# Four probability tiles, two loads moved behind a copy, a gate half copied by GpSimd, and the final scaling issued behind a maximum

## The chip, the cores and the metric

One core of a Trainium2 chip runs the kernel. The metric is the device time of one execution in microseconds. Engines are named as in the profile: PE is TensorE (matmuls; PEld its weight loads), DVE is VectorE, ACT is ScalarE, POOL is GpSimd, and SP is the engine whose queue issues most of the DMAs.

## The reference

One adaLN-modulated layer over 2048 latent tokens of width 1024 with 256 context tokens. All inputs are float32.

```python
h  = rms_norm(x) * (1 + scale) + shift          # scale, shift, gate from silu(c) @ w_ada + b_ada
rq, rk, rv, rg, aq, ak, av, ag = project(h, w_in)    # one combined projection, rope on rq rk aq ak
# group A, 4 heads of 128: retention over chunks of 128, forward (with the diagonal) and backward, summed;
#   y = group_norm(out_f + out_b) * gn_w * silu(rg)
# group B, 8 query heads of 64 on 2 key heads: window of +-128 keys and all 256 context keys, a sink logit:
m = max(max(logits), sink); p = exp(logits - m)
att = (p / (sum(p) + exp(sink - m))) @ v * silu(ag)
x = x + gate * (concat([ret, att]) @ w_out)
return rms_norm(x) * final_norm_w
```

## The kernel before

The first 660 us project all tokens in four groups of 512 and put queries, keys, values, gates and retention states into scratch in DRAM (`d_qkv`, `d_aq`, `d_k`, `d_v`, `d_g`, `d_st`). The work that this document is about comes after: a loop over 16 blocks of 128 tokens, two steps to a block, one for each group of four query heads (`kv` 0 and 1; step t is block t // 2, kv t % 2).

What happens to one attention head (`att_head`, `att_norm`, `att_t`, `att_v`): PE computes its scores S, 128 queries by up to 640 keys, into the single buffer of the pool `pS`. DVE adds the mask and takes the row maximum in one instruction (L759; listed as ISA in the instruction order and as CUSTOM_DVE in the profile), writing the scores to a tile `p` in SBUF. ACT takes the exponential with the row sum (L768), DVE the reciprocal (L777), POOL scales (L778), and a DMA on SP's queue (L782) copies the tile into `pr`, which holds four heads; the change calls this the copy. One step later PE transposes `pr` (L1212) into banks of tag t, ACT and DVE split each bank into a high and a low part `phl` (L1214, L1215), and PE multiplies by the values (`o`, L1225). In names such as `p_1_3` the first number is kv and the second the head in it; `S_0` to `S_7` number all eight heads of a block. The heads of a step belong to the next step's attention, so scores run one step ahead.

The other pieces of a step are retention (`ret_queries` on POOL, `ret_scores`, `ret_values`, `ret_moments`, `ret_norm`, `ret_rows`, `ret_out`), the output projection in eight pieces (`piece`, `proj`: three matmuls for each of the four slices of a half, L1262, then the residual sum by DVE, L1267), `att_out` (ACT's `ob`, DVE's `mf`, POOL's `ma`), `final_sum` (ACT squares the residual row, POOL makes the reciprocal root `rz`) and `final` (DVE scales by `rz` and the norm weights, L1286, and SP stores). `STEPS` lists the pieces of an even and an odd step in program order: a head's scores are a0 to a3, their scaling N0 to N3, transposes T, values V, projection o0 to o7, final sum f, final scaling F0 and F1. A scheduler reorders instructions of an engine around that list by its own priorities; a block under `behind(i)` keeps its instructions after `i` on the engine of `i`. Every engine then works through its own list strictly in that order, SP's queue of DMAs too.

At the hand-over, the last projection unit `ag1` of group 0 runs with the eight heads and the retention of block 0 woven into it (`WEAVE`). Its two results are copied out of PSUM into `glast` so that the projection's PSUM banks become free for the loop's (L1191); `last_gate` later applies silu to `glast`, stores it to `d_g`, and reads a quarter of it back as the upper half of block 0's gate `GA[0]`. `load_qkv`, `load_st`, `load_gr`, `load_kv`, `load_att` and `load_late` (gate `ga` and residual input `xb`) prefetch for later blocks, and `fw` holds the final norm's weights.

Of the kernel before, what the change touches and what calls it, by code (L numbers as in the profile page):

```python
# [8 lines left out]
F32 = mybir.dt.float32  # L9
F32R = mybir.dt.float32r  # L10
BF16 = mybir.dt.bfloat16
AF = mybir.ActivationFunctionType
ALU = mybir.AluOpType
# [3 lines left out]
P = 128  # L17
# [5 lines left out]
GT = 512  # L23
# [4 lines left out]

STEPS = (
    "a0 o0 O o1 a1 N0 o2 T0 r0 T1 r1 U a2 N1 V0 o3 T2 Y V1 o4 a3 N2 T3 V2 o5 q T4 N3 o6 V3 S o7 f V4",  # L30
    "a0 o0 O o1 a1 N0 R T0 F0 F1 a2 N1 T1 B V0 o2 T2 V1 a3 N2 o3 T3 o4 V2 T4 N3 r2 o5 V3 o6 o7 V4",
)
FIRST = "T0 Y T1 V0 T2 V1 q T3 V2 T4 G V3 S V4"

# [5 lines left out]
def tile_hymba(  # L40
# [17 lines left out]
    nc = tc.nc  # L58
    act, dve, pool, pe = nc.scalar, nc.vector, nc.gpsimd, nc.tensor

    const = ctx.enter_context(tc.tile_pool(name="const", bufs=1))
    dram = ctx.enter_context(tc.tile_pool(name="scratch", bufs=1, space=DRAM))

    d_qkv = dram.tile([NB, P, 3, RH, P], F32, name="d_qkv")
# [3 lines left out]
    d_g = dram.tile([NB, P, 2, RH, P], F32, name="d_g")  # L68
# [3 lines left out]
    make_identity(nc, ident)  # L72
    identr = const.tile([P, P], F32R, name="identr")
    dve.tensor_copy(identr, ident)
    ones = const.tile([P, P], F32, name="ones")
    dve.memset(ones, 1.0)

# [29 lines left out]
    def rounded(dst, src, eng="pool"):  # L109
        if eng == "pool":  # L110
            pool.tensor_scalar(dst, src, 1.0, 0.0, op0=ALU.mult, op1=ALU.add)  # L111
        elif eng == "act":
            act.activation(dst, src, AF.Copy)
        else:
            dve.tensor_copy(dst, src)  # L115
# [12 lines left out]
    pr1 = ExitStack()  # L128
    ptp = pr1.enter_context(tc.tile_pool(name="ptp", bufs=3, space=PSUM, side="right"))
    ld = pr1.enter_context(tc.tile_pool(name="ld", bufs=7, side="right"))  # L130

    def tmp(name, shape=(P, GT), dt=F32):
        return tp.tile(list(shape), dt, tag="t", name=name)
# [6 lines left out]
    def lnexp():  # L140
        tc.keep_in_program_order(act.preload_act_table_set("natural_log_exp_and_others"))
# [10 lines left out]
    PE = {}  # L152
# [63 lines left out]
    def behind(i):  # L216
        return tc.issue_after(i.ins) if i else nullcontext()
# [115 lines left out]
    def cols_by_tok(w, c0, ht, n, name, side=False, at={}, pin=False):  # L333
        ps = (ptp if side else pacc).tile([P, GT], F32, tag="tp" if side else "acc", name=name)[:, :n]
        for k in range(NK):
            for f in at.get(k, ()):
                f()
            with tc.issue_after(PE["S"].ins) if pin else nullcontext():
                for i, (a, b) in enumerate(PASSES):
                    pe.matmul(  # L340
                        ps,
                        w[:, a, k, c0 : c0 + P],
                        ht[b][:, k, :],
                        start=(k == 0 and i == 0),
                        stop=(k == NK - 1 and i == 2),
                    )
        return ps
# [62 lines left out]
    def flush():  # L410
        while later:
            later.pop(0)()
# [246 lines left out]
    C2 = {}  # L659

    def window(b):
        slots = sorted((x % 3, x) for x in (b - 1, b, b + 1) if 0 <= x < NB)
        return slots, [x - b + 1 for _, x in slots]
# [4 lines left out]
    def mask_at(b):  # L668
        want = tuple(window(b)[1]) + (1, 1)
        return next(i for i in range(len(MASKS)) if MASKS[i : i + len(want)] == want)  # L670

    VW, QKV, ST, AQ, GR, GA, XB, MR, MA, PB, RF, RT = ({} for _ in range(12))
# [14 lines left out]
    def load_qkv(b):  # L687
        if b < NB:
            QKV[b] = l2.tile([P, 3, RH, P], F32, tag="qkv", name=f"qkv{b}")
            nc.sync.dma_start(QKV[b], d_qkv[b])  # L690

    def load_st(b):
        if b < NB:
# [25 lines left out]
    def tiles_late(b):  # L719
        GA[b] = l2.tile([P, RH, P], F32, tag="ga", name=f"ga{b}")  # L720
        XB[b] = l2.tile([P, D], F32, tag="xb", name=f"xb{b}")

    def load_late(b):
        if b >= NB:
            return
        tiles_late(b)
        if b:
            nc.sync.dma_start(GA[b], d_g[b, :, 1])
        else:
            nc.sync.dma_start(GA[b][:, 0:2], d_g[b, :, 1, 0:2])  # L730
        nc.sync.dma_start(XB[b], xn[b * P : (b + 1) * P, :])


    def att_head(b, kv, j):
        slots = window(b)[0]
        nl = len(slots) * P
        n = nl + CTX
        o = 512 - nl
        h = 4 * kv + j
        ksel = {0: slice(0, 2), NB - 1: slice(0, 3, 2)}.get(b, slice(0, 3))  # L740
        m0 = mask_at(b)
        mk = C2["msk"][:, m0 : m0 + n // P].rearrange("p s t -> p (s t)")
        if j == 0:
            PB[(b, kv)] = (
                C2["pool"].tile([P, 4, 640], F32R, tag="pr", name=f"pr{b}_{kv}"),
                C2["pool"].tile([P, 3, 4], F32, tag="m4", name=f"m4{b}_{kv}"),
                [C2["pool"].tile([P, 641], F32, tag="pb", name=f"p{b}_{kv}_{i}", bufs=3) for i in range(4)],
            )
        _, m4, pbs = PB[(b, kv)]
        pb = pbs[j]  # L750
        psc = pS.tile([P, 1024], F32, tag="S", name=f"S{b}_{h}")
        for hl in range(2):
            i = pe.matmul(  # L753
                psc[:, o:512].rearrange("p (s t) -> p s t", t=P),
                AQ[b][:, h, :], C2["kwin"][:, kv, hl, ksel], start=(hl == 0), stop=(hl == 1),
            )
            pe.matmul(psc[:, 512:768], AQ[b][:, h, :], C2["kctx"][:, kv, hl], start=(hl == 0), stop=(hl == 1))  # L757
        PE["S"] = i
        i = dve.tensor_tensor_reduce(  # L759
            out=pb[:, 0:n], in0=psc[:, o : o + n], in1=mk, op0=ALU.add, op1=ALU.max,  # L760
            scale=1.0, scalar=-3e38, accum_out=m4[:, 0, j : j + 1],
        )
        with behind(i):
            dve.tensor_copy(pb[:, n : n + 1], sink8[:, h : h + 1])  # L764
        dve.tensor_scalar(  # L765
            m4[:, 1, j : j + 1], m4[:, 0, j : j + 1], -0.125, nsink[:, h : h + 1], op0=ALU.mult, op1=ALU.min
        )
        act.activation(  # L768
            pb[:, 0 : n + 1], pb[:, 0 : n + 1], AF.Exp, bias=m4[:, 1, j : j + 1], scale=0.125,
            accum_out=m4[:, 2, j : j + 1],  # L770
        )

    def att_norm(b, kv, j):
        n = len(window(b)[0]) * P + CTX
        pr_, m4, pbs = PB[(b, kv)]
        pb = pbs[j]
        dve.reciprocal(m4[:, 2, j : j + 1], m4[:, 2, j : j + 1])  # L777
        PE["norm"] = pool.tensor_scalar(  # L778
            pb[:, 0:n], pb[:, 0:n], m4[:, 2, j : j + 1], 0.0, op0=ALU.mult, op1=ALU.add
        )  # L780

        nc.sync.dma_start(pr_[:, j, 0:n].bitcast(F32), pb[:, 0:n])  # L782

    BANKS = {"o": 1, "z": 2, "t": 3}

# [271 lines left out]
    r2 = s2g.spread()  # L1057
    ps = [cols_by_tok(wa, c * P, H[3], GT, f"aq03{c}") for c in range(2)]
# [127 lines left out]
    ps = []  # L1186
    for c, weave in enumerate(WEAVE):
        at = {int(w[0]): [jobs[x] for x in w[1:]] for w in weave.split()}
        ps.append(cols_by_tok(wb, c * P, H[0], GT, f"ag10{c}", at=at, pin=True))
    for i in range(2):  # L1190
        dve.tensor_copy(C2["glast"][:, i], ps[i])  # L1191
    flush()
    p1.close()

# [3 lines left out]
    s2 = ctx.enter_context(tc.tile_pool(name="s2", bufs=2, reuse_waits="tile"))  # L1198
    pw = ctx.enter_context(tc.tile_pool(name="pw", bufs=1, space=PSUM, reuse_waits="tile"))
    vctx = C2["vctx"]  # L1200
    fw = s2.tile([P, D], F32, name="fw", bufs=1)
# [27 lines left out]
    def att_out(b, kv):  # L1229
        if kv == 0:  # L1230
            MA[b] = s2.tile([P, 2, RH, P], F32R, tag="ma", name=f"ma{b}")
        ob = s2.tile([64, 4, P], F32, tag="ob", name=f"ob{b}_{kv}", bufs=1)
        act.activation(ob, PO[kv][64:128], AF.Copy)  # L1233
        mf = s2.tile([P, 2, P], F32, tag="mf", name=f"mf{b}_{kv}")
        for q in range(2):
            dve.tensor_tensor(mf[64 * q : 64 * q + 64], PO[kv][0:64, q::2, :], ob[:, q::2, :], op=ALU.add)  # L1236
        ks = slice(2 * kv, 2 * kv + 2)
        dve.tensor_tensor(mf, mf, GA[b][:, ks], op=ALU.mult)
        rounded(MA[b][:, 0, ks, :], mf)
        pool.tensor_tensor(MA[b][:, 1, ks, :], mf, MA[b][:, 0, ks, :], op=ALU.subtract)  # L1240
# [35 lines left out]
    RZ = {}  # L1276
# [6 lines left out]

    def final(b, n):
        x = XB[b][:, n * GT : (n + 1) * GT]
        dve.scalar_tensor_tensor(x, x, RZ[b], fw[:, n * GT : (n + 1) * GT], op0=ALU.mult, op1=ALU.mult)  # L1286
        nc.sync.dma_start(out[b * P : (b + 1) * P, n * GT : (n + 1) * GT], x)

    def last(b):
# [20 lines left out]
    def last_gate():  # L1310

        tc.keep_in_program_order(act.preload_act_table_set("silu_and_others"))
        for i in range(2):
            do_gate(1, 2 + i, 0, C2["glast"][:, i], True, t=C2["glast"][:, i])
        lnexp()
        nc.sync.dma_start(GA[0][:, 2:4], d_g[0, :, 1, 2:4])

    load_gr(0)
    load_late(0)
    load_qkv(1)  # L1320
    load_st(1)
    load_gr(1)
    load_att(1)
    for t in range(2 * NB):
        b, kv = t // 2, t % 2
# [142 lines left out]
```

## Time and profile before

| what | value |
|---|---|
| runs | 1164.23 us median of 3 (1164.11 to 1166.5) |
| profiled execution | 1164.85 us, span of the instructions 1163.1 us |
| PE busy | 1128.2 us (97%) |
| DVE, ACT, POOL busy | 793.8, 470.0, 332.8 us |
| mean granted PE clock | 0.989 |
| DMA moved | 224.38 MB, mean 193 GB/s |

The profile is one execution, with every instruction's start and duration. Idle time of an engine is listed with what ended it. Busy time of PE is modelled from pipelined matmuls, so a single matmul shows about 0.39 us where the next one follows after 0.23. "Granted clock" is the share of full speed that PE was given. DMA rows show the issue on the queue; the time to landing is listed apart.

### The profile page before, as it was taken

To read this page: it belongs to the slowest core of one execution; us is meant where nothing else is said; L and a number is where in the kernel's file an instruction comes from. 1 tells how busy PE (TensorE), PEld (TensorE's weight loads), DVE (VectorE), ACT (ScalarE), POOL (GpSimd) and SP (SyncE) were. 2 spreads that over 40 slices of the span, in tenths; PEclk is the share of its full clock that TensorE was granted. 3 is DMA by queue.
4 is the path that set the end of the run, shared out by engine and by line. 5 is a ranking of instruction groups with operands and counts; after the bars stand their busy time and mean duration, and the time that the engine had idled before them with its cause. 6 is when DMAs were issued, how large, how long until landed. Compare 5 with 4: busy or idle time off the path is not lost. (4 is left out here: it accounts for less than half of the span.)

```text
span 1163.1 us, 18715 instructions
## 1 busy us (share of the span) xinstructions
PE 1128.2 (97%) x6317; PEld 963.0 (83%) x6318; DVE 793.8 (68%) x2028; ACT 470.0 (40%) x1032; POOL 332.8 (29%) x427
## 2 busy tenths in 40 slices
PE   8999999999999999999999987999999999999997
PEld 5877889989888889988888866788888888888885
DVE  7873984655566455665666354788888888888884
ACT  4444422242443013321111342555555555555553
POOL 0000020100012000011032333455555555555552
PEclk9999999999999999999999998899999999999999
DMA  9948893375675333443365466666666666666531
GB/s 338 339 137 267 288 299 101 113 267 141 198 248 173 112 109 120 135 132 96 110 207 168 128 225 205 206 212 226 221 225 228 226 223 222 225 226 224 186 143 67
DMA packets 158551, 224.38 MB, mean 193 GB/s; under 512 B 13299, under 2 KB 105203, under 8 KB 158326
## 3 DMA queue, kind: packets, MB, share of 16 engines
q1 hardware_dynamic: 143380, 215.54, 56.1%
q10 hardware_dynamic: 15074, 7.64, 2.2%
q8 instruction: 50, 0.82, 0.3%
q14 instruction: 47, 0.39, 0.1%
HBM read 130.19 MB, written 50.86 MB: 156 GB/s over the span
## 5 line engine op out<-in xcount | busy, mean ns | idle before, releaser
L768 ACT ACTIVATE p<-p,m 128x641 f32<-128x641 f32 (+1 forms) x128 | 104.6, 817 | 91.7 <-DVE m L765 49.4
L778 POOL TENSOR_SCALAR p<-p,m 128x640 f32<-128x640 f32 (+1 forms) x128 | 106.9, 837 | 115.5 <-DVE m L777 73.5
L1215 DVE TENSOR_TENSOR phl<-pt,phl 128x512 fp32r<-128x512 f32 x156 | 106.8, 686 | 23.6 <-ACT phl L1214 22.2
L759 DVE CUSTOM_DVE_ANT_0 p<-S,msk 128x640 f32<-128x640 f32 (+1 forms) x128 | 102.3, 799 | 9.5 <-PE S L757 5.1
L1214 ACT ACTIVATE phl<-pt 128x512 fp32r<-128x512 f32 x156 | 91.0, 592 | 42.1 <-PE pt L1212 37.1
L1262 PE MATMUL pz<-wg1h,ma 128*128 128x512 f32 x256 | 98.7, 411 | 0.4 <-POOL ma L1240 0.3
L1262 PE MATMUL pz<-wg0h,mr 128*128 128x512 f32 x256 | 97.3, 403 | 1.6 <-DVE mr L115 1.6
L753 PE MATMUL S<-kwin,aq 128*128 128x384 f32 (+1 forms) x256 | 86.9, 359 | 7.2 <-DVE p L764 5.2
L1212 PEld LDWEIGHTS pt<-identr,pr 128*128 128x128 f32 x624 | 69.2, 142 | 16.9 <-DVE glast L1191 2.6
L1225 PE MATMUL o<-phl,vwin 128*128 128x512 f32 x184 | 75.1, 438 | 5.2 <-ACT phl L1214 3.9
L445 ACT ACTIVATE vw<-v,wdec 128x128 fp32r<-128x128 f32 x128 | 43.7, 394 | 85.1 <-DVE v L458 85.1
L1212 PE MATMUL pt<-identr,pr 128*128 128x128 f32 x624 | 73.2, 244 | 3.6 <-DVE glast L1191 2.2
L757 PE MATMUL S<-kctx,aq 128*128 128x256 f32 x256 | 72.1, 285 | 0.0
L753 PEld LDWEIGHTS S<-kwin,aq 128*128 128x128 f32 x256 | 49.1, 192 | 13.3 <-issue 5.4
L1262 PEld LDWEIGHTS pz<-wg0h,mr 128*128 128x128 f32 x256 | 47.9, 188 | 10.1 <-DVE mr L115 1.9
L1262 PEld LDWEIGHTS pz<-wg1h,ma 128*128 128x128 f32 x256 | 48.0, 188 | 7.7 <-POOL ma L1240 1.2
L757 PEld LDWEIGHTS S<-kctx,aq 128*128 128x128 f32 x256 | 49.6, 194 | 2.9
L1262 PE MATMUL pz<-wg1l,ma 128*128 128x512 f32 x128 | 50.5, 394 | 0.0
L1262 PE MATMUL pz<-wg0l,mr 128*128 128x512 f32 x128 | 50.2, 392 | 0.0
L1225 PEld LDWEIGHTS o<-phl,vwin 128*128 128x128 f32 x184 | 34.7, 192 | 16.4 <-ACT phl L1214 6.8
L1225 PE MATMUL o<-phl,vctx 128*128 128x512 f32 x128 | 44.8, 410 | 0.3 <-DVE phl L1215 0.2
L447 DVE SCALAR_TENSOR_TENSOR vw<-v,wdec,vw 128x128 fp32r<-128x128 f32 x128 | 40.4, 360 | 6.8 <-ACT vw L445 6.7
(425 smaller groups left out, 3025.0 us busy)
## 6 DMA issues: line engine op xcount, KB each, us to landing
pr<-p SPq DMA_DIRECT2D x112, 320.0 KB, 3.1
wss<-in_wss SPq DMA_DIRECT2D x32, 512.0 KB, 6.9
qkv<-d_qkv SPq DMA_DIRECT2D x15, 768.0 KB, 5.6
aq<-d_aq SPq DMA_DIRECT2D x64, 128.0 KB, 2.9
xb<-in_xn SPq DMA_DIRECT2D x16, 512.0 KB, 4.0
out<-xb SPq DMA_DIRECT2D x31, 256.0 KB, 2.6
st<-d_st SPq DMA_DIRECT2D x15, 512.0 KB, 3.4
d_g<-g ACTq DMA_DIRECT2D x28, 256.0 KB, 2.8
```

Of the source, the lines that this page charges most:

```text
L445: act.activation(vw[0][:, hh, dr, :], x, AF.Copy, scale=w)
L447: dve.scalar_tensor_tensor(vw[1][:, hh, dr, :], x, w, vw[0][:, hh, dr, :], op0=ALU.mult, op1=ALU.subtract)
L753: i = pe.matmul(psc[:, o:512].rearrange("p (s t) -> p s t", t=P), AQ[b][:, h, :], C2["kwin"][:, kv, hl, ksel], start=(hl == 0), stop=(hl = ...
L757: pe.matmul(psc[:, 512:768], AQ[b][:, h, :], C2["kctx"][:, kv, hl], start=(hl == 0), stop=(hl == 1))
L759: i = dve.tensor_tensor_reduce(out=pb[:, 0:n], in0=psc[:, o : o + n], in1=mk, op0=ALU.add, op1=ALU.max, scale=1.0, scalar=-3e38, accum_out ...
L768: act.activation(pb[:, 0 : n + 1], pb[:, 0 : n + 1], AF.Exp, bias=m4[:, 1, j : j + 1], scale=0.125, accum_out=m4[:, 2, j : j + 1],)
L778: PE["norm"] = pool.tensor_scalar(pb[:, 0:n], pb[:, 0:n], m4[:, 2, j : j + 1], 0.0, op0=ALU.mult, op1=ALU.add)
L1212: pe.transpose(ppt[:, j].bitcast(F32R), pb[:, j, kt * P : (kt + 1) * P], identr)
L1214: PE["phl"] = act.activation(phl[:, 0], ppt, AF.Copy)
L1215: PE["low"] = dve.tensor_tensor(phl[:, 1], ppt, phl[:, 0], op=ALU.subtract)
L1225: pe.matmul(PO[kv], vt, PH[kt][:, hl], start=(kt == 0 and hl == 0), stop=(kt == nkt - 1 and hl == 1))
L1262: PE["prod"] = pe.matmul(PZ[n2], m[:, a, k % RH, :], WG[k // 4][c][:, k % 4, s], start=(k == 0 and i == 0), stop=(k == NK - 1 and i == 2),)
```

## The change

Six edits, acting at or after the hand-over:

- The tile `p` of a head's probabilities gets four buffers in place of three. To make room, `mf` gets one buffer in place of two, and the constant `ones` moves into a pool that is released before the loop.
- From block 2 on, the loads of `qkv` and `xb` are kept behind the latest copy of a head in SP's queue.
- The second `glast` tile is copied by ACT, not DVE.
- The upper half of block 0's gate is copied by POOL from `glast`, not read back by a DMA.
- The final scaling is kept behind the latest maximum in DVE's list.
- In the odd step, projection piece o2 comes ahead of V0.

```diff
-    ... T1 B V0 o2 T2 V1 a3 ...                      # odd step of STEPS
+    ... T1 B o2 V0 T2 V1 a3 ...
-    ones = const.tile([P, P], F32, name="ones")
+    ones = ld.tile([P, P], F32, name="ones", bufs=1)
...
     def load_qkv(b):
-            nc.sync.dma_start(QKV[b], d_qkv[b])
+            with behind(PE["copy"] if b > 1 else None):
+                nc.sync.dma_start(QKV[b], d_qkv[b])
...
     def load_late(b):
-        nc.sync.dma_start(XB[b], xn[b * P : (b + 1) * P, :])
+        with behind(PE["copy"] if b > 1 else None):
+            nc.sync.dma_start(XB[b], xn[b * P : (b + 1) * P, :])
...
     def att_head(b, kv, j):
-                [C2["pool"].tile([P, 641], F32, tag="pb", name=f"p{b}_{kv}_{i}", bufs=3) for i in range(4)],
+                [C2["pool"].tile([P, 641], F32, tag="pb", name=f"p{b}_{kv}_{i}", bufs=4) for i in range(4)],
-        i = dve.tensor_tensor_reduce(
+        i = PE["max"] = dve.tensor_tensor_reduce(
...
     def att_norm(b, kv, j):
-        nc.sync.dma_start(pr_[:, j, 0:n].bitcast(F32), pb[:, 0:n])
+        PE["copy"] = nc.sync.dma_start(pr_[:, j, 0:n].bitcast(F32), pb[:, 0:n])
...
-    for i in range(2):
-        dve.tensor_copy(C2["glast"][:, i], ps[i])
+    dve.tensor_copy(C2["glast"][:, 0], ps[0])
+    act.activation(C2["glast"][:, 1], ps[1], AF.Copy)
...
-        mf = s2.tile([P, 2, P], F32, tag="mf", name=f"mf{b}_{kv}")
+        mf = s2.tile([P, 2, P], F32, tag="mf", name=f"mf{b}_{kv}", bufs=1)
...
     def final(b, n):
-        dve.scalar_tensor_tensor(x, x, RZ[b], fw[:, n * GT : (n + 1) * GT], op0=ALU.mult, op1=ALU.mult)
+        with behind(PE["max"]):
+            dve.scalar_tensor_tensor(x, x, RZ[b], fw[:, n * GT : (n + 1) * GT], op0=ALU.mult, op1=ALU.mult)
...
     def last_gate():
-        nc.sync.dma_start(GA[0][:, 2:4], d_g[0, :, 1, 2:4])
+        pool.tensor_copy(GA[0][:, 2:4], C2["glast"][:, :, 0:P])
```

The edits also shift what the scheduler does around them. Three places, each as it stands in the list of one engine. The line numbers of the new kernel are one to three higher.

The first is DVE at the end of block 0 (steps 1 and 2), before. `xb_6434` is the residual row of block 0, `p_0_3` the last head of block 1's first group, `p_1_0` the next head, `mf_1` and `ga` the gated attention output, `rz` the reciprocal root, `m` the heads' small statistics:

```order
L1236 TENSOR_TENSOR mf_1_6714<-o_1_6630,ob_1_6712 64x256 x2
L1238 TENSOR_TENSOR mf_1_6714<-mf_1_6714,ga_6433 128x256
L777 RECIPROCAL m_0_6535<-m_0_6535 128x1
L1267 TENSOR_TENSOR xb_6434<-pz_0_6549,xb_6434 128x512
L1267 TENSOR_TENSOR xb_6434<-pz_1_6669,xb_6434 128x512
L1286 SCALAR_TENSOR_TENSOR xb_6434<-xb_6434,rz_6865,fw 128x512 x2
L759 ISA p_0_3_6539,m_0_6535<-S_3_6646,msk 128x640
```

and after:

```order
L1238 TENSOR_TENSOR mf_1_6714<-o_1_6633,ob_1_6712 64x256 x2
L761 ISA p_0_3_6539,m_0_6535<-S_3_6646,msk 128x640
L761 ISA m_0_6535 128x1
L766 COPY p_0_3_6539<-sink_83 128x1
L779 RECIPROCAL m_0_6535<-m_0_6535 128x1
L767 TENSOR_SCALAR m_0_6535<-m_0_6535,nsink 128x1
L1240 TENSOR_TENSOR mf_1_6714<-mf_1_6714,ga_6433 128x256
L779 RECIPROCAL m_0_6535<-m_0_6535 128x1
L835 SCALAR_TENSOR_TENSOR ra_6629<-mv_6620,ra_6629 128x4
L1269 TENSOR_TENSOR xb_6434<-pz_0_6549,xb_6434 128x512
L1269 TENSOR_TENSOR xb_6434<-pz_1_6669,xb_6434 128x512
L761 ISA p_1_0_6696,m_1_6695<-S_4_6700,msk 128x640
```

The maximum of `p_0_3` moves ahead of the gating and of both residual sums, and the two scalings leave this stretch. On PE the scores `S_4` move from behind all projection matmuls of block 0 into the middle of them. In every later block the two scalings, which stood on either side of the maximum of `p_0_1`, both follow it.

The second is ACT at the hand-over, before (`first` holds retention rows of block 0, `ra` their group-norm factors, `ag` the last projection's PSUM bank):

```order
L817 ACTIVATE first<-y_6350 128x512
L768 ACTIVATE p_1_3_6293,m_1_6289<-p_1_3_6293,m_1_6289 128x513
L840 ACTIVATE first<-first,ra 128x128 x4
L1214 ACTIVATE phl_0_0_6455<-pt_0_0_6450 128x512
L1214 ACTIVATE phl_0_1_6472<-pt_0_1_6467 128x512
```

and after:

```order
L819 ACTIVATE first<-y_6350 128x512
L842 ACTIVATE first<-first,ra 128x128 x4
L770 ACTIVATE p_1_3_6293,m_1_6289<-p_1_3_6293,m_1_6289 128x513
L1193 ACTIVATE glast<-ag_6287 128x512
L1216 ACTIVATE phl_0_0_6455<-pt_0_0_6450 128x512
```

The gate copy comes in behind the four row scalings and the last exponential, which change places; on DVE the statistics of all four retention heads now precede the last maximum. SP issues `fw` ahead of the last copy there, no longer between that copy and `gr`, and POOL takes the query products `qd` (behind the new gate copy) ahead of `ma`, no longer behind it.

The third is SP's queue in a later block (the same rows recur in each), before:

```order
L782 DMA pr_0_7980<-p_0_0_7982 128x640
L1287 DMA out<-xb_7247 128x512 x2
L782 DMA pr_0_7980<-p_0_1_7983 128x640
L782 DMA pr_0_7980<-p_0_2_7984 128x640
L731 DMA xb_7977<-in_xn 128x1024
L690 DMA qkv_8152<-d_qkv 128x1536
L782 DMA pr_0_7980<-p_0_3_7985 128x640
L679 DMA kwin<-d_k 64x2x128 x2
```

and after:

```order
L784 DMA pr_0_7980<-p_0_0_7982 128x640
L1290 DMA out<-xb_7247 128x512 x2
L784 DMA pr_0_7980<-p_0_1_7983 128x640
L679 DMA kwin<-d_k 64x2x128 x2
L733 DMA xb_7977<-in_xn 128x1024
L784 DMA pr_0_7980<-p_0_2_7984 128x640
L784 DMA pr_0_7980<-p_0_3_7985 128x640
L691 DMA qkv_8152<-d_qkv 128x1536
```

The load of `qkv` goes behind the fourth copy, and two `kwin` loads and the load of `xb` come ahead of the third.

More of the change, by code (lines that the diff above doesn't have):

```diff
@@ L30 @@
     "a0 o0 O o1 a1 N0 o2 T0 r0 T1 r1 U a2 N1 V0 o3 T2 Y V1 o4 a3 N2 T3 V2 o5 q T4 N3 o6 V3 S o7 f V4",
-    "a0 o0 O o1 a1 N0 R T0 F0 F1 a2 N1 T1 B V0 o2 T2 V1 a3 N2 o3 T3 o4 V2 T4 N3 r2 o5 V3 o6 o7 V4",
+    "a0 o0 O o1 a1 N0 R T0 F0 F1 a2 N1 T1 B o2 V0 T2 V1 a3 N2 o3 T3 o4 V2 T4 N3 r2 o5 V3 o6 o7 V4",
 )
@@ L74, in tile_hymba @@
     dve.tensor_copy(identr, ident)
-    ones = const.tile([P, P], F32, name="ones")
-    dve.memset(ones, 1.0)
     pr = const.tile([P, 54], F32, name="pr")
@@ L130, in tile_hymba @@
     ld = pr1.enter_context(tc.tile_pool(name="ld", bufs=7, side="right"))
+    ones = ld.tile([P, P], F32, name="ones", bufs=1)
+    dve.memset(ones, 1.0)
     def tmp(name, shape=(P, GT), dt=F32):
```

## The prediction

> **What bounds the kernel now.** I read the page first, then the busy time by stage, then whom TensorE (PE) waits for, and last the timeline where it waits.
>
> ```profile
> span 1163.1 us, 18715 instructions
> PE 1128.2 (97%) x6317; PEld 963.0 (83%) x6318; DVE 793.8 (68%) x2028; ACT 470.0 (40%) x1032; POOL 332.8 (29%) x427
> ```
>
> PE is busy for 97% of the span, and the change removes no matmul, so only PE's idle time and its slow time can be won. By stage (stretch and its length, busy time with counts for PE, weight loads, DVE, ACT and POOL, then granted clock, DMA share, GB/s):
>
> ```profile
> 718.00:747.00 29.00, 21.08 (x112) 17.91 (x113) 18.63 (x59) 13.94 (x29) 12.54 (x17) 0.76 0.46 160
> 747.00:1110.00 363.00, 359.57 (x2219) 312.14 (x2218) 294.90 (x950) 213.17 (x444) 200.07 (x252) 1.00 0.66 222
> ```
>
> From 747 us on the block loop is bound by PE: 3.4 us idle in 363. The loss is in its start: from 718 to 747 PE idles for 7.9 us, at a mean clock of 0.76. PE's waits from 660 us to the end (waiter, releaser: total us, times, longest):
>
> ```profile
> PE S L753 <- DVE p L764: 5.2, 2, 5.0
> PE o L1225 <- ACT phl L1214: 3.9, 14, 0.6
> PE pt L1212 <- DVE glast L1191: 2.2, 1, 2.2
> PE S L753 <- DVE m L759: 1.9, 2, 1.0
> ...
> PE pt L1212 <- DMA pr<-p: 1.3, 3, 0.8
> PE y L813 <- POOL qd L798: 0.8, 1, 0.8
> PE y L814 <- POOL qd L798: 0.8, 2, 0.5
> ```
>
> The first row is one wait of 5.0 us. The timeline there (start, duration, engine, line, operation; in brackets the idle time before it and what ended it):
>
> ```profile
> 717.77 0.69 DVE L1267 TENSOR_TENSOR xb<-pz,xb 128x512 f32<-128x512 f32 x1 [0.67 <-PE pz L1262]
> 720.06 0.57 POOL L120 TENSOR_TENSOR rz<-rz,half 128x1 f32<-128x1 f32 x1
> 720.66 1.42 DVE L1286 SCALAR_TENSOR_TENSOR xb<-xb,rz,fw 128x512 f32<-128x512 f32 x2 [2.20 <-DMA st<-d_st]
> 722.00 0.82 DVE L759 CUSTOM_DVE_ANT_0 p<-S,msk 128x640 f32<-128x640 f32 x1
> 722.97 0.66 PE L753 MATMUL S<-kwin,aq 128*128 128x384 f32 x1 [5.03 <-DVE p L764]
> ```
>
> The scores S have one buffer in PSUM, so PE cannot write the next head's scores until DVE has taken the maximum of this one's (722.00). DVE works in order, and the two final scalings of block 0 (720.66) stand ahead of that maximum. They need rz, and rz needs the second residual sum (717.77), ACT's squares of it and GpSimd's power (until 720.63). The profile names the load of st as what ended DVE's idle time; but rz, which the scaling reads, ended 0.03 us before it.
>
> The clock there and at the start of the loop, in steps of 3.4 us whose edges are the instants at which it changes:
>
> ```profile
> 683.30:686.70 3.40, 1.24 (x7) 0.69 (x5) 1.99 (x11) 1.46 (x4) 1.29 (x2) 1.00 0.48 157
> 686.70:690.10 3.40, 3.40 (x19) 2.85 (x19) 1.37 (x2) 2.08 (x5) 0.69 (x1) 0.50 0.43 110
> ...
> 693.50:696.90 3.40, 2.32 (x10) 1.94 (x11) 2.49 (x5) 2.52 (x4) 0.00 (x0) 1.00 1.02 416
> 717.40:720.80 3.40, 0.54 (x5) 0.31 (x3) 0.83 (x2) 1.15 (x2) 0.81 (x2) 1.00 0.77 311
> 720.80:724.20 3.40, 1.23 (x5) 1.26 (x6) 2.36 (x7) 0.92 (x2) 0.00 (x0) 0.50 0.00 0
> 724.20:727.60 3.40, 2.33 (x11) 1.74 (x9) 1.92 (x9) 0.58 (x1) 2.08 (x3) 0.50 0.31 115
> 727.60:731.00 3.40, 2.82 (x10) 2.58 (x11) 2.13 (x11) 2.96 (x8) 1.60 (x2) 0.50 0.26 98
> 731.00:734.40 3.40, 3.40 (x13) 2.71 (x12) 2.47 (x9) 2.21 (x6) 0.00 (x0) 0.50 0.66 215
> ```
>
> A step in which PE was busy for 36% (683.3) or 16% (717.4) is followed by one at half clock; one with 68% (693.5) is not, since nothing later up to 717.4 is slow. Half clock ended only after a full step (731.0); 83% (727.6) did not end it. So the wait costs 5.0 us and then four steps, 13.6 us, at half clock.
>
> **The change, part by part.** *Final scaling behind the last maximum.* In the new order head 3's maximum stands ahead of the residual sums and needs nothing of them, and the scalings of block 0 come a block later. The 5.03 us go. Late next is the following head's maximum, which still stands behind both sums: the second ends at 718.46, the maximum takes 0.82, done at 719.3. PE's work ahead of it ended at 717.94 (722.97 less 5.03); with one head's S moved in front (0.6, below) it arrives at 718.6 and waits 0.7. For the two heads after it, S and maximum alternate at 0.6 + 0.8 and some 0.1 of latency, 1.5 us a head, with S itself (0.6) and some transposes (0.3 on average) to fill: two waits of 0.6. New waits 1.9; the same heads' waits that vanish are what PE idles now in the steps 724.2 and 727.6, 1.07 and 0.58. Net −5.0 + 1.9 − 1.65 = −4.75, taken as −4.7.
>
> *The clock.* PE is busy for 9.8 us of the four slow steps (1.23 + 2.33 + 2.82 + 3.40). If all of that is bound by PE, full clock gives back half of it, 4.9; if DVE's pace is the bound, nothing. The last two steps are the nearest to the first case (83% and full), the first two to the second. I take −3.5, bounds 0 and −4.9.
>
> [...]
>
> *Projection step o2 ahead of V0.* Each later block loses a little at one place; the last row is from the chain of waits:
>
> ```profile
> 799.94 0.75 DVE L1286 SCALAR_TENSOR_TENSOR xb<-xb,rz,fw 128x512 f32<-128x512 f32 x1
> 802.50 0.41 PE L753 MATMUL S<-kwin,aq 128*128 128x384 f32 x1
> 803.16 0.46 PE L1212 MATMUL pt<-identr,pr 128*128 128x128 f32 x4
> 803.20 1.11 ACT L1214 ACTIVATE phl<-pt 128x512 fp32r<-128x512 f32 x2
> 803.85 0.19 PEld L1225 LDWEIGHTS o<-phl,vwin 128*128 128x128 f32 x1 [0.38 <-ACT phl L1214]
> ...
> 804.35 0.69 PE pz L1262 x3
> ```
>
> (The four matmuls of one head's S run from 802.50 to 803.16, the 0.6 above.) PE waits for ACT's copy phl of the transposed probabilities, and the three projection matmuls of o2, 0.69 us, stand behind that wait and need nothing of it. They go in front and cover it. Besides, the scaling of 0.75 no longer delays the maximum and exponential that stand ahead of phl on DVE and ACT. The longest of these waits, 0.6, is below 0.69. There are 13 in the PE-bound stretch: I take its whole idle time, −3.4; by the weight loads' wait, 0.38, it could be −4.9.
>
> *The hand-over from projection to block loop: fourth tile, second gate copy on ACT, GpSimd's copy of the gate.*
>
> ```profile
> 684.54 0.72 ACT L768 ACTIVATE p<-p,m 128x513 f32<-128x513 f32 x1 [2.04 <-issue]
> 685.88 0.68 DVE L1191 COPY glast<-ag 128x512 f32<-128x512 f32 x1
> 686.05 1.65 ACT L840 ACTIVATE first<-first,ra 128x128 f32<-128x128 f32 x4 [0.70 <-DVE ra L833]
> 693.37 0.69 DVE L1248 TENSOR_TENSOR gr<-yt,gr 128x512 f32<-128x512 f32 x1 [0.97 <-DMA gr<-d_g]
> 697.48 0.41 POOL L111 TENSOR_SCALAR ma<-mf 128x256 fp32r<-128x256 f32 x1 [10.06 <-DVE mf L1238]
> 698.66 2.50 POOL L798 TENSOR_TENSOR qd<-qkv,decq 128x512 f32<-128x512 f32 x2
> ```
>
> PE's first transpose needs the bank that the second gate copy (glast, until 686.56) empties. That copy moves to ACT, where the four row scalings (1.65) and the last exponential (0.72 and 0.2 for its sum) now stand ahead of it; it takes 0.56 there (phl's rate, 1.11 for two). The scalings start sooner: by 0.9 because heads no longer wait for a copy to free a tile (PE's wait on S of 1.0), by 0.7 because the last maximum no longer stands among the statistics, by 0.7 because the exponential ahead of ACT's copy of y is earlier: 683.75. The copy then ends at 683.75 + 1.65 + 0.92 + 0.56 = 686.9: +0.35, bounds −1.2 and +2.2. The gate load gr is no longer queued behind fw, so DVE's wait of 0.97 goes: −0.9. qd comes ahead of ma on GpSimd: it starts when its load is there and no longer at 698.66 behind ma (from 697.48), and PE's two waits for it (1.6) shrink: −1.2, bounds 0 and −1.6. GpSimd's new gate copy stands ahead of qd; at ma's 0.41 for the same 128x256 it lies in the 10.06 us in which GpSimd idles. Together −1.75, bounds −3.7 and +2.2.
>
> *Loads behind the last copy* are worth nothing by themselves: PE waited for a copy (pr<-p) 1.3 us in all. What they may cost is the last rival. Where ones lies and the single mf buffer meet none of PE's waits: 0.
>
> **Sum**, against the profiled execution of 1164.85 us (span 1163.1 and 1.75 around it; the median of the three runs is 0.6 lower, 1164.23): −4.7 − 3.5 − 3.4 − 1.75 = −13.35, so 1151.5. With every bound at its best (−5.0 − 4.9 − 4.9 − 3.7) it is 1146.3.
>
> **Rivals.** *The clock drops all the same.* My waits of 0.7, 0.6 and 0.6 lie in two or three steps after 718, and would leave PE busy for 65 to 80% of each; a little more waiting than that falls between the 36% that lost the clock and the 68% that kept it. Then the −3.5 goes and the 1.9 of waits doubles with S at half rate: 1155 to 1157.
>
> *The hand-over gets longer.* If the scalings start at 686.05 as now, the copy ends at 686.05 + 1.65 + 0.92 + 0.56 = 689.2; PE waits 2.6 us more and may get a second step at half clock. With the 1.75 lost too: 1155.9. For it: a pipeline of GpSimd, DVE and ACT steps stands ahead of the copy. Against: all four statistics now precede the last maximum.
>
> *The change does not do what it says.* Head 3's maximum may wait for something else and PE's 5.0 stay, clock and all: −3.4 − 1.75, 1159.7. Against it: with four tiles its slot was emptied a whole step before.
>
> *Slower: SP's queue.* In the new order the load xb stands ahead of the copies of heads 2 and 3, and it waits until the output stores of its buffer have landed:
>
> ```profile
> 804.74 3.25 SPq L782 DMA_DIRECT2D pr<-p  x2
> 810.39 0.47 SPq L782 DMA_DIRECT2D pr<-p  x1
> out<-xb SPq DMA_DIRECT2D x31, 256.0 KB, 2.6
> ...
> 815.53 0.64 PE pt L1212 x8
> ```
>
> The stores are issued right ahead of 804.74 and land 2.6 later, at 807.3; the copy of head 2 now ends its issue at 807.99. The copy of head 3 (810.39) is the last that the next transposes (815.53) need. So xb may come some 2 us later than that before head 3's copy moves at all. Beyond that, if the copy's landing has no slack, a microsecond costs 13, one a block: stores that land 3 us later, after 5.6, would eat the gain, and later ones make the kernel slower (1168 at 6 us).
>
> **How the numbers follow.** My forecast, every term near its place (1146 to 1154): 0.52. Clock drop 0.20, longer hand-over 0.12, the stall stays 0.06, slower by the queue 0.05, and 0.05 for mixtures that end near zero. The range 1146 to 1160 takes in the first four, of which some lie beyond its ends. The chances follow: faster 0.90, same 0.05, slower 0.05, where 0.2% (2.3 us) is about what a measurement here can tell from no change.
>
> **What would show it.** Right: no wait over 2 us on S after 715, a granted clock of 1.0 from 715 to 735, the row of o behind phl down from 3.9 to below 1, PE's wait for glast now on ACT and near 3 us with the last projection matmul at 683.6 for 684.5, gr without a wait for its load, qd ahead of ma. Wrong: a stretch at half clock after 715, a wait of PE for glast beyond 4 us, or PE waiting for pr<-p in every block.

## The result and the profile after

The changed kernel takes 1150.72 us (median of four runs, 1149.1 to 1151.66), the kernel before 1164.17 (four runs, 1162.5 to 1166.5). The ratio is 0.9882, with a 95% interval of 0.9861 to 0.9902: 13.5 us faster. The forecast was 1151.5, which is 13.35 less than the profiled execution before (1164.85). The profiled execution after took 1151.11 us, 13.7 less. Its totals:

```profile
span 1149.3 us, 18707 instructions
PE 1122.4 (98%) x6317; PEld 960.0 (84%) x6318; DVE 799.5 (70%) x2027; ACT 470.6 (41%) x1033; POOL 330.4 (29%) x428
```

PE's busy time fell by 5.8 us with the same 6317 matmuls. More than half of that (3.22) lies in the second stretch below, where the clock rose. Another 1.25 lies in the 13 steady blocks, at the same full clock; PE's waits for ACT's `phl` there, 13 of them and 3.4 us in all between 755 and 1130 us, are gone, but that they account for it was not shown. To see where the 13.8 us of the span went, I cut both traces at the same events: PE's first S of block 0 (664.15 before, 664.30 after), the first product with `ma` (710.55, 708.56) and the first `yt` of block 1 (732.05, 722.86). The stretches of the kernel before (length, busy time and counts of PE, weight loads, DVE, ACT and POOL, granted clock, DMA share, GB/s), with a stretch of 375 us inside the steady blocks as third row:

```profile
664.15:710.55 46.40, 40.23 (x232) 33.00 (x231) 24.64 (x88) 21.60 (x41) 13.74 (x17) 0.96 0.73 238
710.55:732.05 21.50, 14.52 (x61) 11.75 (x60) 10.48 (x35) 8.17 (x19) 7.15 (x11) 0.74 0.41 151
755.00:1130.00 375.00, 371.01 (x2299) 322.54 (x2298) 305.30 (x982) 219.07 (x457) 207.01 (x260) 1.00 0.64 216
```

and of the changed kernel:

```profile
664.30:708.56 44.26, 39.83 (x233) 33.40 (x232) 25.00 (x88) 22.24 (x42) 14.39 (x18) 0.96 0.77 246
708.56:722.86 14.30, 11.30 (x60) 8.73 (x58) 8.17 (x33) 6.96 (x15) 7.43 (x11) 1.00 0.47 168
755.00:1130.00 375.00, 374.66 (x2326) 326.37 (x2326) 312.99 (x985) 222.29 (x463) 207.45 (x268) 1.00 0.64 216
```

In the second row PE's idle time falls from 6.98 us to 3.00, and its busy time from 14.52 to 11.30, because the clock is 1.00 and not 0.74. In the third PE idles 0.34 us in 375, where it idled 3.99. PE's waits from 660 us to the end, the six longest rows:

```profile
PE pt L1214 <- ACT glast L1193: 3.3, 1, 3.3
PE pt L1214 <- DMA pr<-p: 2.2, 3, 1.5
PE S L755 <- DVE p L766: 1.7, 1, 1.7
PE o L1227 <- DVE phl L1217: 1.2, 3, 0.8
PE S L755 <- DVE m L761: 1.2, 2, 0.7
PE pz L1264 <- DVE mr L113: 0.6, 1, 0.6
```

The wait of 5.0 for S and the 14 waits of `o` for ACT's `phl` are gone. The timeline of DVE at the place of the old stall, with PE's last projection matmul of block 0, the transposes behind it and the next S:

```profile
715.84 0.40 PE L1264 MATMUL pz<-wg1h,ma 128*128 128x512 f32 x1
715.88 0.16 DVE L835 SCALAR_TENSOR_TENSOR ra<-mv,ra 128x4 f32<-128x4 f32 x1 [3.26 <-POOL ra L118]
715.96 1.29 DVE L1269 TENSOR_TENSOR xb<-pz,xb 128x512 f32<-128x512 f32 x2
716.08 0.37 PE L1214 MATMUL pt<-identr,pr 128*128 128x128 f32 x3
717.16 0.81 DVE L761 CUSTOM_DVE_ANT_0 p<-S,msk 128x640 f32<-128x640 f32 x1
718.13 0.41 PE L755 MATMUL S<-kwin,aq 128*128 128x384 f32 x1 [1.69 <-DVE p L766]
733.15 2.07 DVE L1289 SCALAR_TENSOR_TENSOR xb<-xb,rz,fw 128x512 f32<-128x512 f32 x2
```

The scalings run at 733.15, where nobody waits for DVE. The steps of the clock in the hand-over and at the old stall:

```profile
683.42:686.83 3.41, 0.41 (x5) 0.41 (x6) 0.37 (x4) 2.83 (x7) 0.64 (x1) 1.00 0.63 185
686.83:690.25 3.42, 3.42 (x18) 3.10 (x17) 1.38 (x2) 1.65 (x3) 0.05 (x1) 0.50 0.60 197
690.25:693.66 3.41, 2.63 (x11) 1.37 (x10) 2.74 (x5) 2.86 (x5) 0.00 (x0) 1.00 0.87 317
714.14:717.55 3.41, 2.31 (x13) 1.74 (x11) 1.67 (x4) 0.27 (x1) 1.54 (x3) 1.00 0.70 217
717.55:720.97 3.42, 2.37 (x17) 2.12 (x17) 1.95 (x10) 2.50 (x6) 1.63 (x3) 1.00 0.34 140
```

One step at half clock is left in the hand-over; at the old stall PE is busy for 68 and 69% of two steps and keeps its clock. The hand-over itself:

```profile
683.54 1.65 ACT L842 ACTIVATE first<-first,ra 128x128 f32<-128x128 f32 x4 [3.01 <-DVE p L766]
685.10 0.71 ACT L770 ACTIVATE p<-p,m 128x513 f32<-128x513 f32 x1
685.80 0.57 ACT L1193 ACTIVATE glast<-ag 128x512 f32<-128x512 f32 x1
686.42 0.54 PE L1214 MATMUL pt<-identr,pr 128*128 128x128 f32 x4 [3.28 <-ACT glast L1193]
```

PE ends the projection at 683.14 and waits for ACT, which does four row scalings and an exponential first. And one wait has grown, in block 1: PE waits 1.54 us for the copy of the fourth head, where the kernel before waited 0.20 (SP's queue, and PE's transposes of that head):

```profile
742.30 0.53 SPq L733 DMA_DIRECT2D xb<-in_xn  x1
742.92 0.47 SPq L784 DMA_DIRECT2D pr<-p  x1
743.52 0.51 SPq L691 DMA_DIRECT2D qkv<-d_qkv  x1
749.52 0.63 PE L1214 MATMUL pt<-identr,pr 128*128 128x128 f32 x5 [1.54 <-DMA pr<-p]
```

The fourth head's copy was issued between two large loads, and PE got it 6.6 us after the issue.

### The profile page after: what moved, and what is told of

Its sections match the earlier page's. It is cut to its first block, busy times and chain, and to the rows that moved or that the text cites. A ratio compares the mean times of both kernels' runs of the same rounds, so it can differ in the third digit from the quotient of the medians.

```text
span 1149.3 us, 18707 instructions
## 1 busy us (share of the span) xinstructions
PE 1122.4 (98%) x6317; PEld 960.0 (84%) x6318; DVE 799.5 (70%) x2027; ACT 470.6 (41%) x1033; POOL 330.4 (29%) x428
## 4 chain that ended last, share of the span: by engine, by line
PE 81%; DVE 7%; issue 5%; DMA 3%; POOL 2%; ACT 2%; POOLq 0%; DVEq 0%
PE pz L1264 14%; PE rk L340 7%; PE ag L340 7%; PE rv L353 7%; PE o L1227 6%; PE aq L340 5%; PE S L755 4%; PE rg L340 4%; PE pt L1214 4%; PE rq L340 4%; PE S L759 2%; PE av L340 2%; PE ak L340 2%; PE u L469 2%; DVE wss L214 1%
## 5 line engine op out<-in xcount | busy, mean ns | idle before, releaser
L1235 ACT ACTIVATE ob<-o 64x512 f32<-64x512 f32 x32 | 19.1, 596 | 61.7 <-PE o L1227 61.7
```

## The experiments

Each timed kernel is compared with runs of the kernel before on the same chip, so the ratios are what to compare (the changed kernel's is 0.9882). The stages are read from one profile each, cut as above: A first S of block 0 to first product of `ma`, B to `yt` of block 1, C to `yt` of block 2, D the 13 blocks to `yt` of block 15. The last column is the time at half clock in A and B. No edit acts before the hand-over, and yet the first S of block 0 comes at 660.5 to 664.4 us in these profiles, so it is the stages of a profile that are compared here, not its total. The profile of 1 is of an execution 3.7 us above its median, that of 5 of one 2.3 above, and that of 2 of one 1.6 below.

| kernel | ratio, 95% interval | A | B | C | D | half clock |
|---|---|---|---|---|---|---|
| before | 1 | 46.4 | 21.5 | 28.6 | 372.7 | 17.1 |
| changed | 0.9882, 0.9861 to 0.9902 | 44.3 | 14.3 | 29.3 | 367.7 | 3.4 |
| 1 changed, scaling free | 0.9947, 0.9927 to 0.9967 | 44.5 | 19.2 | 31.6 | 371.6 | 17.1 |
| 2 before, scaling behind maximum | 0.9928, 0.9906 to 0.9950 | 46.1 | 17.6 | 28.7 | 368.9 | 10.2 |
| 3 changed, o2 as before | 0.9864, 0.9844 to 0.9885 | 44.3 | 14.3 | 29.2 | 367.8 | 3.4 |
| 4 before, o2 ahead | 0.9995, 0.9980 to 1.0009 | 46.3 | 21.5 | 29.2 | 375.1 | 20.5 |
| 5 changed, second copy on DVE | 0.9878, 0.9853 to 0.9902 | 45.0 | 16.0 | 29.4 | 368.2 | 10.2 |
| 6 changed, loads free | 0.9871, 0.9848 to 0.9894 | 44.8 | 14.3 | 29.3 | 367.7 | 3.4 |
| 7 changed, three tiles | 0.9865, 0.9843 to 0.9888 | 45.7 | 16.6 | 26.9 | 368.1 | 10.2 |
| 8 changed, gate by DMA | 0.9869, 0.9848 to 0.9891 | 45.6 | 14.3 | 29.7 | 367.5 | 6.8 |
| 9 changed, loads at a step's end | 0.9846, 0.9829 to 0.9863 | 46.2 | 14.0 | 27.1 | 367.6 | 10.2 |
| 10 as 9, row scalings on DVE | 0.9834, 0.9815 to 0.9853 | 43.0 | 15.5 | 27.2 | 367.4 | 10.2 |
| 11 before, scaling and four tiles | 0.9881, 0.9864 to 0.9899 | 44.0 | 14.8 | 29.6 | 368.2 | 0 |
| 12 as 10, three tiles, o2 as before | 1.0016, 1.0006 to 1.0026 | 44.6 | 16.5 | 28.4 | 383.5 | 13.7 |

**1. The scaling free again.**

```diff
-        with behind(PE["max"]):
-            dve.scalar_tensor_tensor(x, x, RZ[b], fw[...], ...)
+        dve.scalar_tensor_tensor(x, x, RZ[b], fw[...], ...)
```

> The changed kernel, with the final scaling no longer kept behind the latest maximum. In DVE's list the first scaling of block 0 then stands ahead of the maximum of the next head but one (p_1_0), which in the changed kernel ran at 717.16. rz is ready at 719.43 there. Theory: the stall comes back in another place, though head 3 has its own fourth tile: scaling until 720.1, maximum until 720.9, so PE waits on S until about 721.1 in place of 718.13. That is 3.0 us, and with four steps at half clock 3.5 more: 1150.7 + 6.5 = 1157.2. Rival 1: the four tiles are what removed the stall, 1151. Rival 2: everything that the scaling order had brought goes, the steady blocks' 3.4 too: 1160.6.

Median 1158.85 us against 1165.59 of the kernel before: between the theory's 1157.2 and rival 2's 1160.6. The timeline at the stall shows the place it named:

```profile
719.15 0.57 POOL L118 TENSOR_TENSOR rz<-rz,half 128x1 f32<-128x1 f32 x1
719.76 0.75 DVE L1288 SCALAR_TENSOR_TENSOR xb<-xb,rz,fw 128x512 f32<-128x512 f32 x1 [2.21 <-POOL rz L118]
720.43 0.82 DVE L761 CUSTOM_DVE_ANT_0 p<-S,msk 128x640 f32<-128x640 f32 x1
721.40 0.66 PE L755 MATMUL S<-kwin,aq 128*128 128x384 f32 x1 [4.36 <-DVE p L766]
```

With a fourth tile head 3's maximum has passed, and the scaling stops the next head's instead: 4.4 us and three slow steps in B. Rival 1 is out: four tiles do not remove the stall. And D is 371.6, not 367.7: the steady gain goes too, with o2 still in front. So the mechanism is rival 2's: everything that the scaling's new place had brought goes.

**2. The scaling alone, in the kernel before.** The same edit put into the kernel before.

> The kernel before, with only the final scaling kept behind the latest maximum (three tiles). Head 3's maximum still stands behind both residual sums (until 718.46) and ends at 719.3, so PE's wait of 5.0 becomes about 1.5. Theory: this order alone removes the long stall and the half clock: 3.5 + 3.5 = 7.0, and some part of the steady blocks' 3.4, since the scaling no longer delays a maximum: 1153.8 to 1157.2. Rival 1: without the fourth tile the stall stays: 1164. Rival 2: the stall shrinks but the clock still drops: 1159 to 1161.

Median 1156.4, as the theory had it; rival 1 is out. PE's waits for S, and the step ahead of the half clock:

```profile
PE S L753 <- DVE m L759: 3.0, 3, 1.2
PE S L753 <- DVE p L764: 1.4, 1, 1.4
```

```profile
715.24:718.65 3.41, 1.58 (x14) 1.32 (x12) 2.24 (x7) 1.97 (x4) 1.11 (x3) 1.00 0.72 294
718.65:722.07 3.42, 1.79 (x5) 1.39 (x6) 1.70 (x10) 0.92 (x2) 1.78 (x3) 0.50 0.32 115
```

The wait of 5.0 became 1.4, and D went from 372.7 to 368.9. Rival 2 is half right: the wait of 1.4 and shorter ones beside it left PE busy for 46% of a step, and two steps ran at half clock. The theory had none left, so its time came true with part of rival 2's loss in it.

**3 and 4. o2.** In the changed kernel back behind V0, and alone in the kernel before.

```diff
-    ... T1 B o2 V0 T2 V1 ...
+    ... T1 B V0 o2 T2 V1 ...
```

> The changed kernel with projection piece o2 behind V0 again. Theory, as the prediction has it: o2 is what covers the wait for phl (0.26 a block, 13 blocks): 1150.7 + 3.4 = 1154.1. Rival: the scaling that no longer stands ahead of the maximum has moved phl forward by up to 0.75, more than the 0.26 that was waited, and o2 is not needed: 1150.7, no row of o behind phl of ACT.

> The kernel before, with only projection piece o2 ahead of V0. Theory: the 13 waits for phl vanish, 1164.2 - 3.4 = 1160.8, and the stall of 5.0 and the half clock stay. Rival: PE reaches the next wait sooner and waits there: 1164.2.

In both the rival was right: o2 is worth nothing. Without it D is 367.8 (367.7 with it), and PE is as full as in the changed kernel (third stretch, kernel 3):

```profile
755.00:1130.00 375.00, 374.44 (x2322) 326.42 (x2321) 312.82 (x982) 221.78 (x462) 205.42 (x267) 1.00 0.63 215
```

Alone it does cover the wait for `phl`, but PE then waits for copies in the same stretch; before, that row was 0.5:

```profile
PE pt L1212 <- DMA pr<-p: 3.9, 5, 1.1
```

What ends late in a steady block before the change is the chain of maximum, exponential and copy, which the scaling delays on DVE; o2 only moves PE's wait along it.

**5. The second gate copy back on DVE.**

```diff
-    act.activation(C2["glast"][:, 1], ps[1], AF.Copy)
+    dve.tensor_copy(C2["glast"][:, 1], ps[1])
```

> The changed kernel with the second gate copy (glast) back on DVE. There DVE is free at 683.62 and the copy takes 0.68, so it would end at 684.3, where ACT's ended at 686.37. Theory of the prediction (ACT costs 0.35): the gain is small, 0 to 1 us, because the next step on the path, ACT's first phl, still stands behind the row scalings and the last exponential (until 685.9, now 687.0): 1149.6 to 1150.7. Rival 1: PE's whole wait of 3.3 shrinks to 1.2 and the step at half clock goes too: 2.1 + 1.7, so 1147. Rival 2: qd stands behind ma on POOL again and PE waits for it: 1151 to 1152.

Median 1151.63, ratio 0.9878 against 0.9882: no difference. PE's two waits in question:

```profile
PE y L815 <- POOL qd L800: 1.8, 1, 1.8
PE pt L1214 <- DVE glast L1193: 1.1, 1, 1.1
```

The wait for the copy fell from 3.3 to 1.1, and `qd` stood behind `ma` on POOL again: 1.8. What one edge gave, the others took: PE idles 4.9 us in A, and 4.4 in the changed kernel.

**6, 7, 8. The other parts, undone one by one.** The two `behind(PE["copy"])` on the loads of `qkv` and `xb` taken off; `bufs=3` for the tiles p; the gate's upper half read back by `nc.sync.dma_start(GA[0][:, 2:4], d_g[0, :, 1, 2:4])`.

> The changed kernel without the two edits that keep the loads of qkv and xb behind the latest copy. Theory of the prediction: worth nothing, 1150.7. Rival 1: the wait for pr<-p of 1.5 at 749.5 comes from loads that crowd the copy; without the edits it goes: 1149.2. Rival 2: with the loads ahead of the copies again PE waits for copies in the blocks, as in the kernel with o2 alone (4.8 us of pr<-p): 1153 to 1155.

> The changed kernel with three tiles p in place of four. DVE's list then has both residual sums of block 0 ahead of head 3's maximum, as in the kernel before; the scaling stays a block later. Theory: the fourth tile is worth what the kernel with the scaling alone lacked: PE waits 1.5 more there, a step with less than half of PE's time busy follows and two steps run at half clock (1.7 to 3.4): 1153 to 1156. Rival: the scaling order is all, 1150.7.

> The changed kernel with the upper half of block 0's gate read back by a DMA, not copied by POOL. Theory of the prediction: 0, 1150.7; in the changed kernel the copy was done at 694.4 and its reader started at 696.79. Rival: the store of glast is issued until 694.9, and a load behind it that takes the 2 to 3 us of other loads lands at 697 to 698; the reader is 0.3 to 1 late, and SP's queue behind it too: 1151 to 1152.

Medians 1149.93, 1149.53 and 1150.49: none of the three edits is needed once all the others are there. With the loads free the wait for `pr` stays (1.6), so the theory of "worth nothing" holds and both rivals fall. With three tiles B is 2.3 longer, as expected, with these waits for S:

```profile
PE S L755 <- DVE m L761: 2.5, 3, 1.0
PE S L755 <- DVE p L766: 1.4, 1, 1.4
```

but block 1 (C) is 2.4 shorter: PE's wait for a copy there is 0.5 and not 1.5. So the whole is not measurably slower, and my theory of 1153 to 1156 was wrong.

**11. The scaling and four tiles, without the rest.** The kernel before with the edit of 2, `bufs=4`, and `mf` and `ones` placed to make room.

> The kernel before with the scaling behind the latest maximum and with four tiles p (mf and ones placed as in the changed kernel), without the moved loads, the gate copies and o2. Theory: the fourth tile takes head 3's maximum ahead of the residual sums and is worth the 1.9 us from the first product of ma to the end that the changed kernel with three tiles lost: 1156.4 of the scaling alone less 2, 1154; the rest up to 1150.7 needs the gate copy on ACT, which brings qd ahead of ma (2.4 us of waits for qd now). Rival 1: the two together are already all of the change: 1150 to 1151. Rival 2: the fourth tile adds nothing to the scaling: 1156.4.

Median 1151.12, ratio 0.9881 against 0.9882: rival 1. These two edits alone reach the time of all six, though 7 shows that the fourth tile is not the only way there. From 2 to 11 the ratio falls by 0.0047, some 5.5 us, and the two intervals just miss each other. The reason shows in the profiles: the profile of 2 has 10.2 us at half clock in A and B, that of 11 none, and PE waits 1.5 less for S (2.9 for 4.4).

**9 and 10. A faster version.** In 9 the loads move to the end of a step, behind its four copies; in 10, besides, block 0's row scalings run on DVE, `ma` stays behind `qd`, and `fw` is loaded last.

```diff
-        if kv == 0:
-            load_qkv(b + 2)
...
-            load_late(b + 1)
...
             ops[w[0]](int(w[1:] or 0))
+        if kv:
+            load_late(b + 1)
+        else:
+            load_qkv(b + 2)
```

```diff
+            dve.tensor_scalar(sd[:, h, :], sd[:, h, :], rs[:, h : h + 1], ra[:, 1, h : h + 1], op0=ALU.mult, op1=ALU.add)
```

> The changed kernel with the loads of qkv, ga and xb written at the end of a step, behind that step's four copies, not at its start. In the changed kernel PE waits 1.5 us at 749.5 for a copy that was issued at 742.92, between xb (512 KB, 742.30) and qkv (768 KB, 743.52), and that took some 6.5 us to land. Theory: the loads crowd it; behind the copies they don't, and the wait of 1.5 falls below 0.5: 1149.4. Rival 1: the load only crowds the next step's copies, the wait moves there: 1150.7. Rival 2: ga or xb is late for its reader a step later: 1152 or more.

> The same as the run with the loads at the end of a step, and the hand-over shortened: the four row scalings of block 0's retention run on DVE, not ACT, so that the second gate copy (glast) on ACT stands only behind the last exponential; ma of block 0's first half stays behind qd on POOL; fw is loaded behind the other first loads. Theory: the exponential may start at 683.6 (was 685.10), the copy ends at 685.1 (was 686.37), ACT's first phl starts at 685.6 (was 687.00): 1.3 less, 1148. Rival 1: PE's wait falls under half of a 3.4 us step, the step at half clock goes too: 1146.5. Rival 2: DVE's row scalings are slower than ACT's 0.41 each and yt waits for them: 1149.4.

Median of 9: 1147.63 against 1165.40; its interval still touches the changed kernel's. The wait at 749.5 is gone (C 27.1 for 29.3), and all waits for `pr` together are 0.3. Median of 10: 1145.59, ratio 0.9834 (0.9815 to 0.9853), below the changed kernel's interval. PE's wait for the second copy is down from 3.3:

```profile
PE pt L1218 <- ACT glast L1198: 1.9, 1, 1.9
```

A is 43.0, the shortest of all. The wait fell by 1.4, as the theory's 1.3 had it, and the step at half clock (rival 1) stayed. In time, 9 and 10 can't be told apart: their intervals overlap.

**12. The same with fewer edits.** As 10, with three tiles and o2 behind V0.

> The kernel of the run with row scalings on DVE and loads at the end of a step, but with two of the six edits left out: three tiles p (mf and ones as in the kernel before) and o2 behind V0. Theory: o2 covers nothing since the scaling moved, and four tiles were replaceable when the gate copy runs on ACT (the changed kernel with three tiles was as fast); so this is as fast as with them: 1145.6 to 1147. Rival: with the hand-over shorter, head 3's maximum behind the residual sums is what PE waits for, and a step falls under half busy, so a step or two run at half clock: 1148 to 1150.

Median 1167.16, 0.2% slower than the kernel before: neither theory nor rival. D is 383.5, 1.2 us a block more. PE waits 1.0 for a maximum in every block, and DVE's timeline in one of them shows why:

```profile
PE S L755 <- DVE m L761: 14.7, 15, 1.0
```

```profile
1008.07 0.81 DVE L761 CUSTOM_DVE_ANT_0 p<-S,msk 128x640 f32<-128x640 f32 x1
1013.39 0.16 DVE L835 SCALAR_TENSOR_TENSOR ra<-mv,ra 128x4 f32<-128x4 f32 x1 [2.38 <-POOL ra L120]
1013.51 0.82 DVE L761 CUSTOM_DVE_ANT_0 p<-S,msk 128x640 f32<-128x640 f32 x1
```

It is the old stall in another dress: the next maximum stands behind `ra` (L835), which waits 2.38 us for POOL, and POOL had waited 4.48 us, until 1011.11, for the reciprocal (1010.85) of the head ahead of it. That head's maximum comes 15 instructions after head 2's in DVE's trace, and 11 after it in kernel 10. Since 7 was fast with three tiles, the tiles alone do not do it; whether it is their sum with the moved loads or with o2 was not separated.

## Why the prediction was right

The signs that it named came: the longest wait on S after 715 is 1.69, the clock from 715 to 735 is 1.00, the row of `o` behind ACT's `phl` is gone, and PE waits 3.3 for `glast`, now on ACT. Term by term:

- **The stall, −4.7.** PE's idle time in B fell by 3.98. The long wait went; the new waits were 2.9 (1.69, 0.45, 0.72) and not 1.9. The first was forecast at 0.7, because the step let one head's S (0.6) run between the last projection matmul and PE's next S. In the new list that S stands among the projection matmuls, so it delays the second sum as well. Behind the last of them (715.84, done at 716.24) come only the transposes of 716.08, and PE then waits for nearly the whole second sum and the maximum. `ra`, which waited 3.26 for POOL ahead of the first sum, adds only some 0.3 to that: the second sum started at 716.57.
- **The clock, −3.5.** PE's busy time in B fell by 3.22. The rival that the clock drops all the same did not come true here, with 68% of a step busy; experiment 2 shows how near it was, with 46%. The four executions of the changed kernel were granted a mean clock of 0.993 to 0.995, every execution of the kernel before 0.982 to 0.990.
- **o2, −3.4.** The steady blocks gained 5.04 (D), close to the best bound of −4.9, the one from the weight loads' wait. But the step named the wrong edit: experiments 1 to 4 give it to the scaling (372.7 to 368.9 by it alone, 371.6 without it) and nothing to o2. The sentence beside it, that the scaling of 0.75 no longer delays maximum and exponential, was the cause. That this term came out is in part luck: both edits were made together, and that hid the wrong owner.
- **The hand-over, −1.75.** A fell by 2.14, its idle time by 1.74 (6.17 to 4.43). The copy ended at 686.37 for 686.9, the projection at 683.14 for 683.6, `gr` no longer waited for its load, and the waits for `qd` went from 1.6 to 0.3. But most of it does not need the gate copies, on which the step spent much of its working: kernel 11 has neither of them, and PE idles 4.84 in its A. There PE waits 1.1 for `glast` and 1.3 for `qd`, where the changed kernel waits 3.3 and 0.3.
- **The loads, 0.** They are worth nothing (6), but not for the reason that copies had slack: PE's wait for a copy in block 1 rose to 1.5, C grew by 0.64, and the wait goes when the loads stand behind the copies (9). It does not come from the two edits on the loads, for it is there without them (1.6 in 6, 2.0 in 11), while with them and three tiles it is 0.5 (7). So it comes with the fourth tile, and the sum had no term for it.
- The rest, −0.21, is the end of the kernel. A to the end sum to −13.95 in these two profiles; the first 664 us differ by 0.15.
- **The sum.** It came within 0.5 us of the two profiles (−13.35 for −13.8), closer than its terms. Stall and clock together gave 1.0 less than forecast, the steady blocks 1.6 more, the hand-over 0.4 more, and block 1 took back 0.64. That these cancel is luck.
- **The other rivals.** The longer hand-over and the slow queue did not come: 3.3 for the copy, and 0.3 for all copies from block 2 on. (The queue rival's 1168 should be 1169.7 by its own numbers: 1.4 us beyond the slack at 13 each.) The stall went; with the fourth tile but without the scaling's new place it would have stayed (1).

## What to carry to other kernels

In an engine that works strictly in order, look for the instruction whose input comes from a slow chain through other engines, and put what others wait for ahead of it: one such edit on DVE was worth 0.7%, and the same fault came back in 1 and 12 as soon as the list let it. The wait that 13 blocks shared here belonged to the latest link of the chain behind it; moving the waiting engine's other work in front of it (o2) only changed what it waited for. Undo each edit of a bundle alone, and try the smallest set alone: here five undone one by one changed nothing that could be measured, and two of the six alone gave the whole gain.

## What the chip showed that I had not expected

In these traces PE's clock changes in steps of 3.41 us, and a step that PE fills only to about half may be followed by a slow one. In experiment 6 both outcomes stand side by side, at 51% (busy time of PE is the first number behind the length, the clock the third from the end):

```profile
682.17:685.59 3.42, 1.73 (x13) 1.34 (x13) 0.74 (x2) 2.63 (x7) 0.69 (x1) 1.00 0.36 143
685.59:689.00 3.41, 3.24 (x13) 2.48 (x13) 1.50 (x3) 1.23 (x3) 0.00 (x0) 0.50 0.87 291
712.89:716.31 3.42, 1.74 (x11) 1.39 (x10) 2.36 (x7) 1.18 (x3) 0.80 (x1) 1.00 0.85 299
716.31:719.72 3.41, 2.24 (x18) 1.96 (x17) 2.17 (x11) 2.46 (x6) 1.64 (x4) 1.00 0.07 27
```

Over the 14 profiles from 665 to 760 us, all 11 steps at full clock that PE filled to less than 45% (0 to 43%) lost it, and none over 64% did. From 45 to 64%, 11 lost it and 15 kept it, so the busy time of PE alone does not decide it; what does was not shown. In experiment 2 a wait of 1.4 with shorter ones beside it left a step 46% busy, and two steps at half clock followed; in the kernel before the wait of 5.0 left one 16% busy, and four followed.

The prediction read from one place that half clock ends only after a full step. Over these profiles it ended after steps with 87% (twice), 95%, and 99 to 100%, and went on after steps with 83 to 84% and with 92 to 94%.

The steps lie differently against the program in these profiles. The same wait of 3.3 for the gate copy fell into one step in the changed kernel (3.4 us at half clock), and was cut into two in 8 (6.8) and 9 (10.2; PE idle for 1.54 us of the first step and 1.74 of the second); in 11 the hand-over's waits left every step more than half full, and there was none. That makes stage A 44.3 to 46.2 with one and the same wait, so a difference of one or two us between two single profiles at such a place is no finding. The five executions of kernel 5 differ too, with one program: the mean granted clock was 0.995 in the two that took 1148.5 and 1148.8 us, and 0.990 to 0.991 in the three that took 1151.6 to 1154.0.
